# Attention layer of a decoder trunk: order of the indexer's projections and head pairs, place of the top-k selection, engine of the mask and bias sum

## The chip, the cores and the metric

The kernel runs on one core of one Trainium2 chip. The metric is the time of one execution on the device in microseconds (us), as the median of several runs. Five engines run their own instruction streams in order: PE (TensorE, the matmuls, with PEld for its weight loads), DVE (VectorE), ACT (ScalarE), POOL (GpSimd) and SP (SyncE, which here only issues DMAs).

## What is computed

A trunk of two layers over 256 tokens of width 1024, in float32. Each layer has a half-step SwiGLU network, a mixer, and another half-step SwiGLU network, each behind an RMS norm and added to the residual. The mixer of the first layer is a pooling and convolution module, which the change does not touch. The mixer of the second layer is sparse attention:

```
proj = h @ c_w_in                      # q, k, v (16 heads x 64), qi (8 x 64), ki (64), wi (8)
rel   = relu(einsum('thd,sd->ths', qi, ki))
score = einsum('ths,th->ts', rel, wi) * idx_scale, -inf where s > t
sel   = top_k(score, 64)               # 64 of the causal keys for each query
logits = q . k[sel] * attn_scale + rel_bias[t5_bucket(t - sel)], -inf where sel > t
y = softmax(logits) . v[sel] @ c_w_out
```

The kernel computes the logits of all causal keys and adds a mask that removes the keys that are not among the 64 selected.

## The kernel before

All weights are streamed from memory. One float32 weight tile (`raw`) is split into two parts, `hi` (a rounding to the matmul's input type, made by ACT at L158) and `lo` (the rest, `raw - hi`, made by DVE at L182, in one place by POOL). A product is the sum of three matmuls, hi·hi, hi·lo and lo·hi. There are two kinds of weight tile: `gu` (1024 rows of 256 columns, split in two instructions) and `d` (128 rows of 1024 columns, one instruction). `pump(n)` (L170) writes the splits of the next n tiles of the stream into the instruction streams, where a free buffer is at hand; `issue()` then has SP issue the next loads. The author sets the order by hand: what stands earlier in the code stands earlier on each engine, and no scheduler reorders it.

The second layer's mixer, `mixer_c`, runs in this order:

- `wide` (L292) projects the indexer's queries (items 0 and 1, two banks of 128 columns each, `use_qi`) and its keys and weights (item 2, 72 columns, `use_kw`). Its first pass takes the first 128 tokens of all three, its second pass (L312, L315) finishes item 0, 1, 2 in turn. `use_kw` writes `kw` (64 rows of keys, 8 rows of head weights), and POOL issues a DMA that copies the 64 key rows to rows 64 to 127 of another tile, `k2` (L778).
- The loop over eight chunks of V (L823, twelve matmuls each). Behind chunk 0, `index_weights` transposes the head weights (L793). Behind chunks 1 to 4, `index_heads` (L804) computes the scores of two indexer heads, in a block of four small matmuls over 64 rows. Heads with an even number use rows 0 to 63 and `kw`, heads with an odd number rows 64 to 127 and `k2`. The pairs are (0, 2), (4, 1), (6, 3), (5, 7). ACT takes the relu (L807), DVE sums it into `score` (L811, L813).
- Behind chunk 5, `select` (L954) masks the future with POOL (L958) and then runs eight rounds on DVE; each finds and removes the eight largest scores of each query (L968, L969). L972 turns what was removed into the additive `mask`.
- The loop over eight pairs of attention heads, steps s = 0 to 7. Step s projects q and k of pair s (`qk_group`, L268, two groups of 24 matmuls), between them computes the logits of pair s-1 (`logits`, L873, L875), and at its start transposes the probabilities of pair s-2 (L900), at its end multiplies them with V (L912). The bias of a pair is a tile `bm` that `load_bias` loads with two DMAs of POOL's queue (L858); `mask_bias` adds the mask to it with two POOL instructions (L863, L865). DVE adds the biased mask to the logits and takes the row's extreme (L883), ACT takes the exponential (L885), DVE divides by the sum (L889, L891).

Of the kernel before, what the change touches and what calls it, by code (L numbers as in the profile page):

```python
# [11 lines left out]
ALU = mybir.AluOpType  # L12
# [27 lines left out]
def tile_trunk(ctx: ExitStack, tc: tile.TileContext, d: dict, out: bass.AP):  # L40
# [248 lines left out]
            bvs.append(b.rearrange("p (l n) -> p l n", l=2))  # L289
        return bvs  # L290

    def wide(items, finish_b, pumps=True, ahead=2):  # L292

        banks = []
        for n, (w, cols, _) in enumerate(items):
            if n == len(items) - 1:
                finish_b()
            bs = []
            for cs, tag in cols:
                m = cs.stop - cs.start  # L300
                b = bank(tag)
                bv = b[:m].rearrange("p (l n) -> p l n", l=2)
                for c in range(NCH):
                    pe.matmul(bv[:, :, 0:P], w[0][:, c, cs], hT[:, c, 0:2, 0:P],  # L304
                              start=c == 0, stop=False, skip_group_check=True)
                bs.append((bv, cs))
            banks.append(bs)
        pump(ahead)
        for (w, cols, use), bs in zip(items, banks):
            for bv, cs in bs:  # L310
                for c in range(NCH):
                    pe.matmul(bv[:, :, P:2 * P], w[0][:, c, cs], hT[:, c, 0:2, P:2 * P],  # L312
                              start=False, stop=False, skip_group_check=True)
                for c in range(NCH):
                    pe.matmul(bv[:, 0, :], w[1][:, c, cs], hT[:, c, 0, :],  # L315
                              start=False, stop=c == NCH - 1, skip_group_check=True)
            done("gu")
            use([bv for bv, _ in bs])
            if pumps:
                pump(1)  # L320
# [443 lines left out]
    def mixer_c(finish_b, gname):  # L764
# [11 lines left out]
        def use_kw(bvs):  # L776
            wide_sum(bvs[0], 72, kw)
            pool.dma_start(k2[64:128], kw[0:64])  # L778

        two = (slice(0, P), slice(P, 2 * P))  # L780
        wide([(weights("gu"), list(zip(two, ("g0", "g1"))), use_qi(0)),
              (weights("gu"), list(zip(two, ("g2", "g3"))), use_qi(1)),
              (weights("gu"), [(slice(0, 72), "a0")], use_kw)], finish_b)
        g = load_gain(gname)


# [29 lines left out]
        for c in range(NCH):  # L816
# [7 lines left out]
                                  start=c == 0 and n == 0, stop=c == NCH - 1 and n == 2)  # L824
            if c == 0:
                index_weights()
            if 1 <= c <= 4:
                index_heads(((0, 2), (4, 1), (6, 3), (5, 7))[c - 1])
            if c == 5:
                mask = select(score)  # L830
            pump(2)
            done("d")
        v = [[None, None], [None, None]]
        for t in range(2):
            for half in range(2):
# [24 lines left out]

        def mask_bias(j):
            m = biases[j]
            pool.tensor_tensor(m[:, :, 256:384], m[:, :, P:256],  # L863
                               mask[:, None, 256:384].to_broadcast([P, 2, P]), op=ALU.add)
            pool.tensor_tensor(m[:, :, 0:256], m[:, :, 0:256],  # L865
                               mask[:, None, 0:256].to_broadcast([P, 2, 256]), op=ALU.add)

        def logits(j, tags):
            q, k = qk[j, 0], qk[j, 1]
# [46 lines left out]
            dve.tensor_tensor(lo, b[:, 0:256], f32(hi), op=ALU.subtract)  # L916
            kts[j] = (hi, lo)

        load_bias(0)
        for s in range(8):  # L920
            if s >= 2:
                transposes(s - 2, ("a0", "a1"))
            w = weights("gu")
            b = bank(f"g{s % 2}")
            qk_group(s, w, b, 0)
            if s >= 1:
                if s < 8:
                    load_bias(s)
                mask_bias(s - 1)
                logits(s - 1, ("g2", "g3"))  # L930
            pump(1)
            qk_group(s, w, b if s else bank("g2"), 1)
            done("gu")
            if s >= 2:
                values(s - 2, f"b{s % 2}")
# [5 lines left out]
            pump(1)  # L941
            done("d")

        mask_bias(7)
        out_all(0)
        logits(7, ("g2", "g3"))
        out_all(1)
# [215 lines left out]
```

## Time and profile before

| | us |
|---|---|
| median of three runs | 988.77 (988.34 to 989.34) |
| the profiled execution | 987.02 |
| span of the profiled execution, first to last instruction | 985.3 |
| PE busy in the span | 963.4 (98%) |
| DVE, ACT, POOL busy | 658.6, 534.3, 62.3 |

A busy time says how long an engine had an instruction in work. A PE near 98% means that nearly every microsecond of the kernel is a matmul, and that the few idle stretches and slow stretches of PE are what can be read off the trace one by one. The time of other engines counts only where PE waits for them. The timelines give a start and a duration; PE's instructions overlap, so the cost of a block is read from one start to the next start, not from durations.

### The profile page before, as it was taken

To read this page: it belongs to the slowest core of one execution; us is meant where nothing else is said; L and a number is where in the kernel's file an instruction comes from. 1 tells how busy PE (TensorE), PEld (TensorE's weight loads), DVE (VectorE), ACT (ScalarE), POOL (GpSimd) and SP (SyncE) were. 2 spreads that over 40 slices of the span, in tenths; PEclk is the share of its full clock that TensorE was granted. 3 is DMA by queue.
4 is the path that set the end of the run, shared out by engine and by line. 5 is a ranking of instruction groups with operands and counts; after the bars stand their busy time and mean duration, and the time that the engine had idled before them with its cause. 6 is when DMAs were issued, how large, how long until landed. Compare 5 with 4: busy or idle time off the path is not lost.

```text
span 985.3 us, 14682 instructions
## 1 busy us (share of the span) xinstructions
PE 963.4 (98%) x5720; PEld 836.3 (85%) x5720; DVE 658.6 (67%) x1083; ACT 534.3 (54%) x959; POOL 62.3 (6%) x89
## 2 busy tenths in 40 slices
PE   7999999999979999999999999999999999999997
PEld 6888888898869888888988888888899798888885
DVE  6876666678568666666686666667888658666653
ACT  5665555565556645554565555445556556555542
POOL 3000000000000000000000000000435000000000
PEclk9999999999999999999999999999999999999999
DMA  9875555535246757655365555437444527655401
GB/s 335 305 278 186 191 190 188 187 109 181 65 148 230 264 205 244 237 194 190 111 254 192 192 192 193 162 107 279 148 137 151 210 71 253 232 189 191 155 1 43
DMA packets 38021, 182.03 MB, mean 185 GB/s; under 512 B 6416, under 2 KB 6448, under 8 KB 24768
## 3 DMA queue, kind: packets, MB, share of 16 engines
q1 hardware_dynamic: 32400, 169.92, 48.6%
q0 software_dynamic: 5264, 10.92, 3.4%
q8 instruction: 45, 0.74, 0.3%
q10 hardware_dynamic: 288, 0.27, 0.1%
q14 instruction: 24, 0.20, 0.1%
HBM read 179.92 MB, written 4.22 MB: 187 GB/s over the span
## 4 chain that ended last, share of the span: by engine, by line
PE 92%; DVE 4%; ACT 2%; issue 2%; DMA 0%; POOL 0%; SPq 0%; POOLq 0%; DVEq 0%; ACTq 0%
PE g L284 29%; PE g L287 15%; PE a L341 14%; PE b L341 13%; PE g L268 4%; PE g L312 2%; PE g L315 2%; PE g L304 2%; PE a L268 1%; DVE lo L182 1%; PE b L538 1%; PE a L312 1%; PE a L315 1%; PE b L823 1%; DVE keep L969 1%
## 5 line engine op out<-in xcount | busy, mean ns | idle before, releaser
L182 DVE TENSOR_TENSOR lo<-raw,hi 128x1024 fp32r<-128x1024 f32 (+1 forms) x319 | 380.4, 1244 | 57.8 <-ACT hi L158 57.8
L158 ACT CAST hi<-raw 128x1024 fp32r<-128x1024 f32 x320 | 314.7, 1043 | 5.4 <-DMA raw<-in_c_out 2.6
L284 PE MATMUL g<-hT,hi 128*128 128x512 f32 x1248 | 310.7, 391 | 0.8 <-DVE t L327 0.8
L284 PEld LDWEIGHTS g<-hT,hi 128*128 128x128 f32 x1248 | 228.7, 188 | 44.8 <-DVE t L327 1.0
L324 ACT COPY t<-g 128x256 f32<-128x256 f32 x174 | 63.4, 372 | 222.2 <-PE g L287 205.9
L287 PEld LDWEIGHTS g<-hT,lo 128*128 128x128 f32 x1248 | 170.3, 190 | 12.2
L287 PE MATMUL g<-hT,lo 128*128 128x256 f32 x1248 | 174.0, 282 | 0.0
L327 DVE TENSOR_TENSOR t<-g,t 128x256 f32<-128x256 f32 x174 | 71.9, 421 | 137.2 <-ACT t L324 137.0
L341 PE MATMUL a<-hi,kh 128*128 128x512 f32 x208 | 82.7, 398 | 0.0
L341 PE MATMUL b<-hi,kh 128*128 128x512 f32 x208 | 82.6, 397 | 0.0
L341 PE MATMUL a<-lo,kh 128*128 128x512 f32 x208 | 81.9, 394 | 0.0
L341 PE MATMUL b<-hi,kl 128*128 128x512 f32 x208 | 81.5, 392 | 0.0
L341 PE MATMUL b<-lo,kh 128*128 128x512 f32 x208 | 81.5, 392 | 0.0
L341 PE MATMUL a<-hi,kl 128*128 128x512 f32 x208 | 81.0, 389 | 0.0
L392 ACT CAST kh<-t 128x256 fp32r<-128x256 f32 x88 | 35.7, 406 | 57.8 <-DVE t L390 57.8
L393 DVE TENSOR_TENSOR kl<-t,kh 128x256 fp32r<-128x256 f32 x88 | 37.4, 425 | 41.5 <-ACT kh L392 41.5
L388 ACT ACTIVATE t<-t 128x256 f32<-128x256 f32 x88 | 36.9, 420 | 26.1 <-DVE t L327 26.1
L235 POOL TENSOR_TENSOR sm<-sm,mhalf 128x1 f32<-128x1 f32 x11 | 6.1, 554 | 673.2 <-DVE sm L233 673.2
L341 PEld LDWEIGHTS a<-hi,kl 128*128 128x128 f32 x208 | 39.1, 188 | 8.8
L341 PEld LDWEIGHTS b<-hi,kl 128*128 128x128 f32 x208 | 39.3, 189 | 8.3
L341 PEld LDWEIGHTS b<-hi,kh 128*128 128x128 f32 x208 | 39.4, 189 | 8.2
L341 PEld LDWEIGHTS b<-lo,kh 128*128 128x128 f32 x208 | 39.4, 189 | 7.8
(210 smaller groups left out, 949.9 us busy)
## 6 DMA issues: line engine op xcount, KB each, us to landing
raw<-in_gu SPq DMA_DIRECT2D x87, 1024.0 KB, 4.8
raw<-in_dn SPq DMA_DIRECT2D x88, 512.0 KB, 5.3
raw<-in_c_qk SPq DMA_DIRECT2D x8, 1024.0 KB, 4.9
raw<-in_ab_in SPq DMA_DIRECT2D x6, 1024.0 KB, 4.8
raw<-in_ab_out SPq DMA_DIRECT2D x8, 512.0 KB, 5.2
raw<-in_c_v SPq DMA_DIRECT2D x8, 512.0 KB, 4.3
raw<-in_c_out SPq DMA_DIRECT2D x8, 512.0 KB, 4.0
eall<-escr POOLq DMA_DIRECT2D x4, 768.0 KB, 17.3
```

The lines of the kernel that those rows point to most:

```text
L158: act.copy(hi[:, c], raws[k][:, c])
L182: e.tensor_tensor(lo[:, c], raws[k][:, c], f32(hi[:, c]), op=ALU.subtract)
L268: pe.matmul(dst, wt[:, c, cols], hT[:, c, part, :], start=n == 0, stop=n == len(seq) - 1)
L284: pe.matmul(b, hi[:, c, cols], hT[:, c, 0:2, :], start=c == 0, stop=False, skip_group_check=True)
L287: pe.matmul(b[:, 0:256], lo[:, c, cols], hT[:, c, 0, :], start=False, stop=c == NCH - 1, skip_group_check=True)
L312: pe.matmul(bv[:, :, P:2 * P], w[0][:, c, cs], hT[:, c, 0:2, P:2 * P], start=False, stop=False, skip_group_check=True)
L324: act.copy(t[:m], bv[:, 1, :])
L327: dve.tensor_tensor(dst[:m], bv[:, 0, :], t[:m], op=ALU.add)
L341: pe.matmul(acc, kt[a][:, ts], w[b][:, hs], start=start and n == 0, stop=stop and n == 2)
L388: act.activation(s, gv, AF.Silu)
L392: act.copy(hi, m)
L393: dve.tensor_tensor(lo, m, f32(hi), op=ALU.subtract)
```

## The change

Six edits, all in the second layer's mixer and in `wide`:

1. `wide` gets an order for its second pass, here item 2 (keys and head weights), then 0, then 1. The banks are handed out anew: item 2 has `g0`, and the fourth bank of the queries is `a0`. `done` reports a finished weight tile only when all before it are finished.
2. The head pairs are (0, 1), (2, 3), (4, 5), (6, 7), behind chunks 0 to 3.
3. `select` stands behind chunk 3 and behind that chunk's `pump(2)`; a dummy exponential (`preload`) stands ahead of it on ACT.
4. `mask_bias` runs on DVE. It stands one step earlier: the mask of pair 0 ahead of the loop, that of pair s in step s.
5. The biases of pairs 0 and 1 are loaded ahead of the loop, the bias of pair s+1 in step s, behind the logits.
6. Step 0 splits no weight tile, step 1 splits two.

```diff
-    def wide(items, finish_b, pumps=True, ahead=2):
+    def wide(items, finish_b, pumps=True, ahead=2, second=None):
...
-        for (w, cols, use), bs in zip(items, banks):
+        ended = set()
+        for n in second or range(len(items)):
+            (w, cols, use), bs = items[n], banks[n]
...
-            done("gu")
+            before = next(k for k in range(len(items) + 1) if k not in ended)
+            ended.add(n)
+            done("gu", next(k for k in range(len(items) + 1) if k not in ended) - before)
...
-        wide([(weights("gu"), list(zip(two, ("g0", "g1"))), use_qi(0)),
-              (weights("gu"), list(zip(two, ("g2", "g3"))), use_qi(1)),
-              (weights("gu"), [(slice(0, 72), "a0")], use_kw)], finish_b)
+        wide([(weights("gu"), list(zip(two, ("g1", "g2"))), use_qi(0)),
+              (weights("gu"), list(zip(two, ("g3", "a0"))), use_qi(1)),
+              (weights("gu"), [(slice(0, 72), "g0")], use_kw)], finish_b, second=(2, 0, 1))
...
             if c == 0:
                 index_weights()
-            if 1 <= c <= 4:
-                index_heads(((0, 2), (4, 1), (6, 3), (5, 7))[c - 1])
-            if c == 5:
-                mask = select(score)
+            if c < 4:
+                index_heads((2 * c, 2 * c + 1))
             pump(2)
             done("d")
+            if c == 3:
+                preload(AF.Exp)
+                mask = select(score)
...
         def mask_bias(j):
             m = biases[j]
-            pool.tensor_tensor(m[:, :, 256:384], m[:, :, P:256],
-                               mask[:, None, 256:384].to_broadcast([P, 2, P]), op=ALU.add)
-            pool.tensor_tensor(m[:, :, 0:256], m[:, :, 0:256],
-                               mask[:, None, 0:256].to_broadcast([P, 2, 256]), op=ALU.add)
+            dve.tensor_tensor(m[:, :, 256:384], m[:, :, P:256],
+                              mask[:, None, 256:384].to_broadcast([P, 2, P]), op=ALU.add)
+            dve.tensor_tensor(m[:, :, 0:256], m[:, :, 0:256],
+                              mask[:, None, 0:256].to_broadcast([P, 2, 256]), op=ALU.add)
...
-        load_bias(0)
+        for j in range(2):
+            load_bias(j)
+        mask_bias(0)
         for s in range(8):
...
             if s >= 1:
-                if s < 8:
-                    load_bias(s)
-                mask_bias(s - 1)
                 logits(s - 1, ("g2", "g3"))
-            pump(1)
+                if s < 7:
+                    load_bias(s + 1)
+                pump(2 if s == 1 else 1)
+                mask_bias(s)
             qk_group(s, w, b if s else bank("g2"), 1)
...
-        mask_bias(7)
         out_all(0)
```

On PE, the first block of indexer heads. Before, it stands behind chunk 1 of V (`a0` is that chunk's last bank, `b1` the next chunk's first), and both of its heads read `kw`, rows 0 to 63:

```order
L823 MATMUL a0_1231_6594<-hi_1210_6464,hT_90 128x512
L804 MATMUL g1_1243_6643<-kw_6402,t1_1216_6508 128x256
L804 MATMUL g3_1244_6644<-kw_6402,t1_1217_6511 128x256
L804 MATMUL g1_1243_6643<-kw_6402,t1_1216_6508 128x128
L804 MATMUL g3_1244_6644<-kw_6402,t1_1217_6511 128x128
L823 MATMUL b1_1234_6597<-hi_1213_6470,hT_90 128x512
```

Now it stands behind chunk 0, directly behind the transposes of the head weights:

```order
L827 MATMUL a0_1231_6594<-hi_1185_6317,hT_90 128x512
L797 MATMUL g0_1236_6611<-ident_74,kw_6402 128x8 x2
L808 MATMUL g1_1237_6615<-kw_6402,t1_1220_6534 128x256
L808 MATMUL g2_1238_6616<-k2_6403,t1_1220_6534 128x256
L808 MATMUL g1_1237_6615<-kw_6402,t1_1220_6534 128x128
L808 MATMUL g2_1238_6616<-k2_6403,t1_1220_6534 128x128
L827 MATMUL b1_1234_6597<-hi_1210_6464,hT_90 128x512
```

The block moved up by one chunk, and each of its two heads reads its own half of the rows.

On DVE, from the end of the selection (its last round, then the mask) to the first logits (L883, `bm` is the bias), before:

```order
L969 MATCH_REPLACE keep_6778<-sm_6830,keep_6777 128x128
L972 TENSOR_SCALAR keep_6833<-keep_6778 128x384
L182 TENSOR_TENSOR lo_6849<-raw_6725,hi_6847 128x1024
L182 TENSOR_TENSOR lo_6867<-raw_6757,hi_6865 128x1024
L182 TENSOR_TENSOR lo_6911<-raw_6789,hi_6909 128x1024
L883 ISA t_1316_6980,sm_6984<-g_1314_6974,bm_6879 128x128
```

and now:

```order
L975 MATCH_REPLACE keep_6750<-sm_6802,keep_6749 128x128
L978 TENSOR_SCALAR keep_6805<-keep_6750 128x384
L182 TENSOR_TENSOR lo_6833<-raw_6707,hi_6831 128x1024
L182 TENSOR_TENSOR lo_6851<-raw_6739,hi_6849 128x1024
L182 TENSOR_TENSOR lo_6869<-raw_6761,hi_6867 128x1024
L868 TENSOR_TENSOR bm_6881<-bm_6881,keep_6805 128x2x128
L870 TENSOR_TENSOR bm_6881<-bm_6881,keep_6805 128x2x256
L888 ISA t_1314_6976,sm_6980<-g_1312_6970,bm_6881 128x128
```

Three splits stand between mask and logits as before, and the two sums of mask and bias have joined them.

On ACT, from the relu of the last two indexer heads to the first copy of V, before:

```order
L807 ACTIVATE t_1266_6745<-g_1264_6739 128x384
L807 ACTIVATE t_1267_6749<-g_1265_6740 128x384
L158 CAST hi_6753<-raw_6661 128x1024
L158 CAST hi_6785<-raw_6693 128x1024
L158 CAST hi_6847<-raw_6725 128x1024
L158 CAST hi_6865<-raw_6757 128x1024
L837 COPY v_6871<-a_1231_6594 128x512
```

and now:

```order
L811 ACTIVATE t_1263_6727<-g_1261_6721 128x384
L811 ACTIVATE t_1264_6731<-g_1262_6722 128x384
L158 CAST hi_6735<-raw_6544 128x1024
L258 ACT_TABLE_LOAD
L258 ACTIVATE sm_6741<-mhalf 128x1
L158 CAST hi_6757<-raw_6675 128x1024
L158 CAST hi_6831<-raw_6707 128x1024
L158 CAST hi_6849<-raw_6739 128x1024
L158 CAST hi_6867<-raw_6761 128x1024
L842 COPY v_6873<-a_1231_6594 128x512
```

The table load, which stood ahead of the first exponential (L885), is now here, and the copies of V have one more cast ahead of them.

## Rows read from the trace of the kernel before

**Rows 1.** The page: its span, and the chain that ended last by engine.

```profile
span 985.3 us, 14682 instructions
...
PE 92%; DVE 4%; ACT 2%; issue 2%; DMA 0%; POOL 0%; SPq 0%; POOLq 0%; DVEq 0%; ACTq 0%
```

**Rows 2.** Waits of PE: who waited for whom, total us, times, longest us.

```profile
PE a L900 <- DVE t L891: 2.0, 2, 1.1
```

**Rows 3.** PE's timeline, indexer: start us, us, engine, line, operation, tiles, count.

```profile
661.68 1.37 PE L312 MATMUL g<-hT,hi 128*128 128x256 f32 x8
...
669.61 1.10 PE L312 MATMUL a<-hT,hi 128*72 128x256 f32 x8
...
685.75 0.48 PE L804 MATMUL g<-kw,t 64*128 64x256 f32 x1
685.75 0.48 PE L804 MATMUL g<-k,t 64*128 64x256 f32 x1
...
686.60 0.50 PE L823 MATMUL b<-hi,hT 128*128 128x512 f32 x1
...
689.57 1.57 PE L804 MATMUL g<-k,t 64*128 64x256 f32 x8
691.07 0.50 PE L823 MATMUL b<-hi,hT 128*128 128x512 f32 x1
```

**Rows 4.** PE's timeline, the first steps of the attention loop, and a later one.

```profile
708.09 0.70 PE L873 MATMUL g<-t,t 64*128 64x256 f32 x4
...
719.70 0.70 PE L873 MATMUL g<-t,t 64*128 64x256 f32 x4
...
753.25 0.70 PE L873 MATMUL g<-t,t 64*128 64x256 f32 x4
...
757.16 0.87 PE L912 MATMUL b<-t,v 128*64 128x256 f32 x8
757.96 0.88 PE L900 MATMUL a<-ident,t 128*128 128x128 f32 x6
...
761.63 0.70 PE L873 MATMUL g<-t,t 64*128 64x256 f32 x4
```

**Rows 5.** A stretch: length, busy us of five engines, granted clock, DMA share, GB/s.

```profile
715.20:718.70 3.50, 3.50 (x20) 3.50 (x20) 3.17 (x2) 1.09 (x3) 0.95 (x1) 0.56 0.12 46
```

**Rows 6.** DVE's timeline: selection, first logits, and a later pair.

```profile
694.09 0.41 DVE L968 MAX8 sm<-keep 128x8 f32<-128x256 f32 x1
...
705.78 0.36 DVE L972 TENSOR_SCALAR keep<-keep 128x384 f32<-128x384 f32 x1
706.05 5.13 DVE L182 TENSOR_TENSOR lo<-raw,hi 128x1024 fp32r<-128x1024 f32 x3
711.11 0.28 DVE L883 CUSTOM_DVE_ANT_0 t<-g,bm 128x128 f32<-128x128 f32 x1
...
762.70 0.29 DVE L883 CUSTOM_DVE_ANT_0 t<-g,bm 128x128 f32<-128x128 f32 x1 [0.20 <-PE g L875]
...
765.13 0.55 DVE L891 TENSOR_SCALAR t<-t,sm 128x128 f32<-128x128 f32 x2
```

**Rows 7.** DVE's groups from 676 to 694 us: count, busy us, mean ns, idle before.

```profile
L182 DVE TENSOR_TENSOR lo<-raw,hi 128x1024 fp32r<-128x1024 f32 x8 | 9.6, 1230 | 0.0
```

**Rows 8.** POOL: groups from 690 to 775 us, and the copy of the keys.

```profile
L865 POOL TENSOR_TENSOR bm<-bm,keep 128x512 f32<-128x512 f32 x8 | 13.7, 1716 | 0.7
...
L863 POOL TENSOR_TENSOR bm<-bm,keep 128x256 f32<-128x256 f32 x8 | 7.8, 976 | 7.5 <-DVE keep L972 7.4
...
673.02 0.59 POOL L778 DMA_DIRECT2D k<-kw  x1 [14.27 <-DVE kw L327]
```

**Rows 9.** Time to landing: of the bias loads, and of the copied keys.

```profile
DMA to landing us min/median/max: 2.3/2.6/5.0
...
k<-kw POOLq DMA_DIRECT2D x1, 64.0 KB, 5.1
```

**Rows 10.** ACT's timeline, the last cast ahead of the copies of V.

```profile
697.75 1.05 ACT L158 CAST hi<-raw 128x1024 fp32r<-128x1024 f32 x1 [2.57 <-DMA raw<-in_c_out]
```

## The prediction

> **What bounds the kernel now.** I read the page first: the chain that ended last runs over PE for 92% of the span [rows 1], so a change pays only where it takes time from PE, either instructions or waits. The other engines are read only for whether PE waits for them. The list of PE's waits names one in the part that the change touches: L900, the transposes of the first pair's probabilities, waited 2.0 us in two pieces for DVE's division L891 [rows 2]. PE's timeline shows what this wait costs in all. From the logits of pair 0 to those of pair 1, 708.09 to 719.70, PE took 11.61 us; the same stretch of a later step, 753.25 to 761.63, took 8.38, of which the product with V (757.16 to 757.96, 0.80) is not yet there in the early step. So the early step should take 7.58 and takes 4.03 more [rows 4]. The wait itself is 2.0 of that; behind it the granted clock was 0.56 over 3.5 us [rows 5], which is mostly the lower of the two levels, 1.2 instead of 2.4 GHz. The clock fell behind the idle time and rose again under dense matmuls. A waiting time that goes should take its slow stretch along.
>
> What made DVE late is its own queue [rows 6]: the selection runs from 694.09 to the mask at 706.14, then three splits take 5.13 us, and only at 711.11 comes the first L883, though the logits' matmuls began at 708.09. An undisturbed split is 1.23 us [rows 7], three are 3.7; the other 1.4 fell together with POOL's sums of mask and bias [rows 8].
>
> **The indexer's head pairs.** A block whose two heads share the rows took 689.57 to 691.07, 1.50 us; one with heads from both halves took 685.75 to 686.60, 0.85, and the rows show the two halves starting at the same moment [rows 3]. Two of the four blocks, (0, 2) and (5, 7), are of the first kind and become of the second: 2 x 0.65 = **1.3 us less on PE**, which nothing hides. The trace says nothing on a block directly behind the transposes of the head weights; one interruption of the V chunks goes and one change of matmul shape is new, which I take as 0 (from 0.2 lost to 0.2 won).
>
> The Trainium skill, page "TensorEngine Tiling (Array Packing)", section "Theoretical Speedup", gives up to 2x for a contraction of at most 64 rows. By that a block would fall from 1.50 to 0.75 and the sum would be 1.5; the measured block is at 0.85, so the rows' 1.3 stands.
>
> **Keys first.** The first block now needs `kw` and `k2` one chunk earlier, and it needs `k2`, which the old first block did not. The keys' group moves from 669.61 to the place of 661.68, 7.9 us earlier [rows 3]. So the copying DMA goes from 673.02 to about 665.1 [rows 8], and with its 5.1 us to landing [rows 9] the copy is there at 670.2. The blocks' period is 3.82 (685.75 to 689.57); the last block will begin at 685.95 (0.85 for the new first block, 0.65 less for the second), so the first at 685.95 - 3 x 3.82 = 674.5. The cover is 4.3 us: cost nothing. If the landing took 10 us, PE would wait 0.6. The same groups stand in the same passes, so `wide` itself costs what it did; the gain's DMA behind the copy in POOL's queue goes earlier as well.
>
> **The selection.** From the end of the last block to the first maximum it was 691.07 to 694.09, 3.02 us, with relu, sums and one split between; the same instructions stand there now. The last block ends at 685.95 + 0.85 = 686.8, so the selection starts near 689.8 and, 12.05 long [rows 6], gives the mask at 701.9 instead of 706.1. Three undisturbed splits (3.7) bring DVE to 705.6.
>
> **Mask and bias on DVE.** Eight times two sums, 256 and 512 columns, leave POOL (0.98 and 1.72 in the mean [rows 8]) and join DVE. The trace of before has no such sum on DVE. The nearest row is the split: also a float32 difference of two operands in SBUF, 1.23 for 1024 columns [rows 7]; 768 columns are 0.9 at that rate, and with a second start I take 1.1. The ends are 0.9 and POOL's 2.7. With 1.1 DVE is free at 706.7. PE's first logits come at 708.09 - 1.3 = 706.8, and DVE can take them 1.07 later (761.63 to 762.70 [rows 4, 6]), at 707.9, so DVE waits for PE there and not the other way round. From L883 to the end of the last division it is 2.98 (762.70 to 765.13 + 0.55 [rows 6]): 710.8. PE wants the transposes of the first head 3.91 behind the logits (753.25 to 757.96 less 0.80), at 710.7, those of the second 0.3 later, 711.0. It fits with 0.1 to 0.2 to spare; a wait of up to 0.5 here is the likeliest loss. The stall of **4.0 us goes**, and its slow stretch with it.
>
> Behind the sums in DVE's queue wait the next L883, the division and so PE's next transposes. In step 1 three splits and the sums follow the division: 710.8 + 3.7 + 1.1 = 715.6, against logits at 706.8 + 7.58 + 1.07 = 715.4: 0.2 late, where PE leaves 4.71 - 4.05 = 0.66. In a later step the chain from the logits is 4.05 + 2.5 (two splits) + 0.3 (gaps, an estimate from the 0.20 of idle time ahead of L883 in [rows 6]) + 1.1 + 0.4 (the split of the product) = 8.3, against 9.45 (8.38 + 1.07): cost nothing. This cover is gone from 2.2 us for a pair of sums.
>
> **Bias loads, step 0, ACT.** A bias is now loaded a step ahead of its sum, 8.38 us against landings of 2.3 to 5.0 [rows 9]: nothing. What step 0 doesn't split, step 1 does (counted above). On ACT the table load leaves the place ahead of the first exponential, where ACT waited for DVE anyway. New ahead of the copies of V is one more cast, whose tile can only be loaded when POOL has split an earlier one. Before, the last cast there began at 697.75 after 2.57 us of waiting for a load [rows 10]; one more such wait and cast (2.57 + 1.05) puts the copies at 702.4 at worst, which leaves 4.4 us for the copies of V and of q and k until the logits at 706.8. Cost nothing; if it were 3 us later, the logits would be late by about as much.
>
> **The sum.** 1.3 + 4.0 = 5.3, about 5.4 with half of the interruption: the span goes from 985.3 to 979.9. The profiled execution took 987.02, 1.7 over its span and 1.75 under the median; I take the 5.4 off the median: 988.77 - 5.4 = **983.4**.
>
> **Rivals.**
> - *The wait only moves* (0.18). If the first division is late for another reason than the selection (the three splits waiting for casts, the cast for its load, or the sums nearer to 2.7), part of the 4.0 stays. For: 0.2 us of room is little, and three splits still stand between mask and sums. Against: about 4.2 us of lead on DVE. With half of the stall kept 985.4 (0.08), with all of it 988.77 - 1.3 = 987.5 (0.10).
> - *The pairing brings nothing* (0.05): the first block waits for `k2`, or blocks in the new place take 1.5. Then 4.0 alone: 984.8. Against it: the 4.3 us of cover and the two blocks that already run at 0.85.
> - *DVE becomes the bound of the loop* (0.07), the one that ends slower. Place: the sums ahead of each L883. From 2.2 us a pair each step is late by the excess. At POOL's 2.7 it is 0.5 x 7 - 0.66, about 2.8, and the time 986.2. It turns into a loss (over 2 us above before) from about 3.3 a pair; if each of the two took the 1.72 of POOL's longer group, 3.4, it would be 1.2 x 7 - 0.66 = 7.7, with one slow stretch (3.5 x 0.44 = 1.5) 9.2, so 992.6. For: DVE has the longest chain of the loop and POOL's work is put into it. Against: the same kind of operation at 1.23 for 1024 columns, and POOL no longer lengthens DVE's splits.
> - *It doesn't do what it says*: the selection would have to wait for something that the code doesn't show, such as POOL's masking of the future. That is the first rival's case.
>
> **How the numbers follow.** Forecast 983.4 with 0.70, for itself from 982.5 (0.2 more from the interruption, 0.5 scatter of runs) to 984.4. Under 0.2%, 2 us, a measurement of this kernel can't be told from no change. Faster: 0.70 + 0.08 + 0.05 = 0.83. Same: 0.10. Slower: 0.07. The range takes in the half-kept stall (985.4), the missing pairing (984.8) and sums at POOL's price (986.2): 982.3 to 986.2.
>
> **What would show it.** Right: four indexer blocks at 0.85; the mask near 702; no wait of L900 near 711 and no stretch under full clock there; from logits to logits 7.6 in step 1 and 8.4 later; DVE's sums at 0.3 to 0.7 each. Wrong: L883 of pair 0 later than 708.5; a wait of a block for the key copy near 674.5; steps longer than 8.4; or a stall of PE in a place where it had none.

## The result, and the profile after

The changed kernel took 983.61 us in the median of four runs (982.65 to 984.21) against 989.06 for the kernel before on the same chip (988.34 to 989.44). The ratio is 0.995, with a 95% interval from 0.9937 to 0.9963. The forecast was 983.4. So the time was right; the reason was right in part, as the experiments below show.

The profiled execution of the changed kernel took 983.51 us. Its page answers [rows 1] (first fence). PE's list of waits has one in the mixer that was not there before (second fence):

```profile
span 981.7 us, 14669 instructions
...
PE 94%; DVE 2%; ACT 1%; issue 1%; DMA 1%; SPq 0%; POOL 0%; POOLq 0%; DVEq 0%; ACTq 0%
```

```profile
PE b L345 <- DVE kl L921: 0.3, 1, 0.3
```

The wait of [rows 2] is gone. The chain runs over PE for 94% instead of 92%, over DVE for 2% instead of 4%.

PE's timeline (start us, us, engine, line, operation, tiles, count, and in brackets the idle time ahead and who ended it), the lines that answer [rows 3] and [rows 4], and the new wait; L808, L878 and L905 are the former L804, L873 and L900, and L345 is the output product behind the loop of attention pairs:

```profile
676.07 0.48 PE L808 MATMUL g<-kw,t 64*128 64x256 f32 x1
676.08 0.48 PE L808 MATMUL g<-k,t 64*128 64x256 f32 x1
...
676.92 0.50 PE L827 MATMUL b<-hi,hT 128*128 128x512 f32 x1
...
708.12 0.70 PE L878 MATMUL g<-t,t 64*128 64x256 f32 x4
...
711.95 0.82 PE L905 MATMUL a<-ident,t 128*128 128x128 f32 x6
...
715.56 0.70 PE L878 MATMUL g<-t,t 64*128 64x256 f32 x4
...
723.95 0.70 PE L878 MATMUL g<-t,t 64*128 64x256 f32 x4
...
765.43 0.50 PE L345 MATMUL b<-hi,kh 128*128 128x512 f32 x1 [0.26 <-DVE kl L921]
```

The first block of indexer heads takes 0.85 from start to start (676.07 to 676.92), both halves starting together. From the first logits to the second it is 7.44 (before 11.61), then 8.39. The transposes at 711.95 wait for nothing. The granted clock is full where it was 0.56 in [rows 5]; the columns of this row are its stretch, its length, the busy us of PE, PEld, DVE, ACT and POOL, the granted clock, the DMA share and GB/s:

```profile
712.50:721.00 8.50, 8.50 (x74) 7.75 (x73) 7.87 (x20) 6.91 (x17) 1.06 (x2) 1.00 0.61 224
```

DVE's timeline, which answers [rows 6]: the mask (L978), the three splits, the sums of mask and bias (L868, L870), the first logits (L888), and the last pair's sums ahead of a split of a product (L921):

```profile
703.29 0.36 DVE L978 TENSOR_SCALAR keep<-keep 128x384 f32<-128x384 f32 x1
703.57 3.49 DVE L182 TENSOR_TENSOR lo<-raw,hi 128x1024 fp32r<-128x1024 f32 x3
706.97 0.42 DVE L868 TENSOR_TENSOR bm<-bm,keep 128x256 f32<-128x256 f32 x1
707.43 0.69 DVE L870 TENSOR_TENSOR bm<-bm,keep 128x512 f32<-128x512 f32 x1
...
709.08 0.29 DVE L888 CUSTOM_DVE_ANT_0 t<-g,bm 128x128 f32<-128x128 f32 x1 [0.96 <-PE g L880]
...
763.90 0.42 DVE L868 TENSOR_TENSOR bm<-bm,keep 128x256 f32<-128x256 f32 x1
764.35 0.69 DVE L870 TENSOR_TENSOR bm<-bm,keep 128x512 f32<-128x512 f32 x1
764.96 0.42 DVE L921 TENSOR_TENSOR kl<-b,kh 128x256 fp32r<-128x256 f32 x1
```

DVE now stands idle for 0.96 us ahead of the first logits; before, PE waited for DVE. (The first logits of DVE also start 0.96 behind those of PE, 709.08 less 708.12. The two lengths are equal by chance; it is the second that is compared with other runs below.) Its three splits take 3.49 instead of 5.13, and the two sums 1.07 from the first start to the next instruction's.

Two profiled executions can't be compared by their spans alone: the first large product started at 21.05 us in the profile of before and at 22.57 in this one. So I cut the mixer into three stages by the starts of PE's instructions: the V loop (first matmul of V to the first q group), the attention loop (to the first output matmul) and the output stage (to the next network's first matmul). The same kernel run again repeats these lengths to 0.07 us. us:

| kernel | V loop | attention | output | sum | timed: median, ratio to before (95% interval) |
|---|---|---|---|---|---|
| before | 27.89 | 67.61 | 26.69 | 122.19 | 989.06 |
| after | 26.39 | 63.44 | 27.24 | 117.07 | 983.61, 0.995 (0.9937 to 0.9963) |
| again | 26.39 | 63.44 | 27.31 | 117.14 | 984.01, 0.9952 (0.9939 to 0.9966) |
| u_pairs | 27.65 | 63.44 | 27.31 | 118.40 | 983.94, 0.9957 (0.9944 to 0.9971) |
| u_heads | 26.63 | 63.77 | 27.24 | 117.64 | 984.46, 0.9953 (0.9941 to 0.9965) |
| u_sums | 26.39 | 64.27 | 26.69 | 117.35 | 984.59, 0.9955 (0.9938 to 0.9971) |
| u_heads_sums | 26.63 | 65.23 | 26.69 | 118.55 | 984.65, 0.9954 (0.994 to 0.9969) |
| u_step0 | 26.39 | 65.10 | 27.27 | 118.76 | 985.97, 0.997 (0.9957 to 0.9983) |
| b_dve | 27.89 | 64.69 | 26.71 | 119.29 | 985.75, 0.9968 (0.9955 to 0.9981) |
| late3 | 26.39 | 64.97 | 27.28 | 118.64 | 983.46 (one run; before beside it 987.73) |
| late5 | 26.39 | 68.36 | 27.29 | 122.04 | 987.65 (one run; before beside it 987.95) |
| dose2 | 26.39 | 63.49 | 28.19 | 118.07 | 983.79 (one run; before beside it 987.73) |
| dose3 | 26.39 | 66.07 | 31.71 | 124.17 | 989.44 (one run; before beside it 987.73) |
| v2_sum7_late | 26.39 | 63.44 | 26.71 | 116.54 | 982.92, 0.9937 (0.9924 to 0.9949) |

The change is −1.50 in the V loop, −4.17 in the attention loop and +0.55 in the output stage, −5.12 in all, against −5.45 between the medians. Outside of the three stages nothing moved: from the first large product to the first matmul of V it is 650.43 us before and 650.44 after, and from the next network's first matmul to the end of the span 191.6 in both. So the new order in `wide` costs nothing.

### The profile page after: what moved, and what is told of

Read it like the earlier page. It is cut to its first block, busy times and chain, and to the rows that moved or that the text cites. A ratio compares the mean times of both kernels' runs of the same rounds, so it can differ in the third digit from the quotient of the medians.

```text
span 981.7 us, 14669 instructions
## 1 busy us (share of the span) xinstructions
PE 961.3 (98%) x5720; PEld 834.6 (85%) x5720; DVE 653.1 (67%) x1099; ACT 534.2 (54%) x960; POOL 40.7 (4%) x73
## 4 chain that ended last, share of the span: by engine, by line
PE 94%; DVE 2%; ACT 1%; issue 1%; DMA 1%; SPq 0%; POOL 0%; POOLq 0%; DVEq 0%; ACTq 0%
PE g L284 29%; PE g L287 15%; PE a L345 14%; PE b L345 13%; PE g L268 5%; PE g L314 2%; PE g L317 2%; PE g L304 2%; PE a L268 1%; PE b L827 1%; PE a L827 1%; PE b L542 1%; DVE lo L182 1%; PE a L317 1%; PE a L314 1%
## 5 line engine op out<-in xcount | busy, mean ns | idle before, releaser
L182 DVE TENSOR_TENSOR lo<-raw,hi 128x1024 fp32r<-128x1024 f32 (+1 forms) x319 | 371.6, 1217 | 58.5 <-ACT hi L158 58.2
L345 PE MATMUL b<-hi,kh 128*128 128x512 f32 x208 | 82.7, 397 | 0.3 <-DVE kl L921 0.3
L345 PE MATMUL a<-hi,kh 128*128 128x512 f32 x208 | 82.7, 398 | 0.0
L345 PE MATMUL a<-lo,kh 128*128 128x512 f32 x208 | 81.9, 394 | 0.0
L345 PE MATMUL b<-hi,kl 128*128 128x512 f32 x208 | 81.5, 392 | 0.0
L345 PE MATMUL b<-lo,kh 128*128 128x512 f32 x208 | 81.5, 392 | 0.0
L345 PE MATMUL a<-hi,kl 128*128 128x512 f32 x208 | 81.0, 389 | 0.0
L345 PEld LDWEIGHTS b<-hi,kh 128*128 128x128 f32 x208 | 39.4, 189 | 8.8 <-DVE kl L921 0.7
L345 PEld LDWEIGHTS a<-hi,kl 128*128 128x128 f32 x208 | 39.1, 188 | 8.8
L345 PEld LDWEIGHTS b<-hi,kl 128*128 128x128 f32 x208 | 39.3, 189 | 8.3
L345 PEld LDWEIGHTS b<-lo,kh 128*128 128x128 f32 x208 | 39.4, 189 | 7.8
L394 DVE TENSOR_TENSOR t<-t,t 128x256 f32<-128x256 f32 x88 | 37.4, 425 | 11.7 <-ACT t L392 4.2
```

What stands on the lines that cost most here:

```text
L182: e.tensor_tensor(lo[:, c], raws[k][:, c], f32(hi[:, c]), op=ALU.subtract)
L345: pe.matmul(acc, kt[a][:, ts], w[b][:, hs], start=start and n == 0, stop=stop and n == 2)
L394: dve.tensor_tensor(m, s, uv, op=ALU.mult)
```

## The experiments

The medians of most of these kernels lie within one another's intervals; what tells them apart are the stage lengths, which the table gives. All edits are made to the changed kernel, except in b_dve.

**The changed kernel again**, to learn how far a stage repeats.

> The changed kernel once more, as the yardstick for the other kernels on this chip. Theory (two block costs of 0.65 us and one stall of 4.0 us went, one of about 0.5 us is new): 5.3 us under the kernel before, ratio 0.9945; V loop from its first matmul to the first group of q 26.4 us, attention loop 63.4, output stage 27.2. Rival (part of the gain was the start of the profiled execution): the three lengths differ from these by more than 0.2 us.

The stages came out within 0.07 us of the first profile. A difference of 0.2 in a stage can be read; one of 1 us between two medians can't.

**The old head pairs in the new place.**

```diff
-                index_heads((2 * c, 2 * c + 1))
+                index_heads(((0, 2), (4, 1), (6, 3), (5, 7))[c])
```

> The changed kernel with the old head pairs (0,2), (4,1), (6,3), (5,7) in the new places. Theory: two blocks take 1.50 instead of 0.85 us, V loop 26.4 + 1.3 = 27.7; the selection starts 1.0 to 1.3 later, PE's logits as well, so nothing else changes: total 1.3 over the changed kernel. Rival (the pairing also decides whether DVE is in time): 2 us or more over it, with a wait at the first transposes.

PE's timeline shows the first pair as one row of eight matmuls over the same rows, 1.57 long:

```profile
677.40 1.57 PE L808 MATMUL g<-kw,t 64*128 64x256 f32 x8
```

The V loop is 1.26 longer, and the attention loop the same to 0.01. The pairing is worth what [rows 3] gave for it, 2 x 0.65, and nothing else hangs on it. The timed median didn't show it (983.94): runs of this kernel lay between 983.53 and 986.29.

**Head blocks and selection one chunk later.** The lead of the selection, which the prediction took for the reason that the stall ends, is cut.

```diff
-            if c < 4:
-                index_heads((2 * c, 2 * c + 1))
+            if 1 <= c <= 4:
+                index_heads((2 * c - 2, 2 * c - 1))
...
-            if c == 3:
+            if c == 4:
```

> The changed kernel with the four blocks of indexer heads, and the selection behind them, one chunk later (behind chunks 1 to 4, selection behind chunk 4), all else as changed; one of the three splits behind the mask then stands ahead of the selection. Theory (the lead of one chunk is what removes the stall): selection 2.95 later, less one split of 1.15; DVE takes the first logits 0.7 to 1.0 us late, PE waits that long at the first transposes; if the clock falls as before 2 to 2.5 over the changed kernel, if not about 1. Rival (the stall went because POOL no longer sums): within 0.3 of the changed kernel.

The first logits of DVE came 1.50 behind PE's (708.46), 0.54 later than in the changed kernel, where they come 0.96 behind:

```profile
709.96 0.28 DVE L888 CUSTOM_DVE_ANT_0 t<-g,bm 128x128 f32<-128x128 f32 x1
```

```profile
708.46 0.70 PE L878 MATMUL g<-t,t 64*128 64x256 f32 x4
...
712.29 1.14 PE L905 MATMUL a<-ident,t 128*128 128x128 f32 x6
```

The transposes took 1.14 instead of 0.82, and the attention loop grew by 0.33, less than the wait of 0.7 to 1.0 that I expected. The V loop grew by 0.24. The stall didn't come back: most of what DVE lost here was idle time before. The run moves the selection back by one chunk only, with two splits behind the mask instead of three. The old place, behind chunk 5, is in b_dve.

**The sums back on POOL**, in their new place.

```diff
-            dve.tensor_tensor(m[:, :, 256:384], m[:, :, P:256],
+            pool.tensor_tensor(m[:, :, 256:384], m[:, :, P:256],
...
-            dve.tensor_tensor(m[:, :, 0:256], m[:, :, 0:256],
+            pool.tensor_tensor(m[:, :, 0:256], m[:, :, 0:256],
```

> The changed kernel with the sums of mask and bias on POOL again, in their new places. Lengths from the first matmul of V to the next layer's first: 117.1 us changed, 122.2 before. Theory (several edits each make DVE earlier, and any of them is enough): DVE's three splits behind the mask slow to 5 us, but its first logits have 0.96 us to spare and no sum of 1.07 ahead, so the attention loop stays within 0.3 of 63.4; the output stage falls to 26.7, since no sum stands ahead of the split of pair 5; 116.6 to 117.2. Rival (the move off POOL is what removed the stall): attention loop 66 or more.

The attention loop lost 0.83. DVE was in time for the first logits (it still stood idle for 0.52 ahead of them), as expected, but, as I had not expected, its second division fell together with POOL's next sum and took 1.47 (for two instructions), where the first took 0.55. The three views, DVE, POOL and PE:

```profile
710.21 0.55 DVE L896 TENSOR_SCALAR t<-t,sm 128x128 f32<-128x128 f32 x2
...
711.10 1.47 DVE L896 TENSOR_SCALAR t<-t,sm 128x128 f32<-128x128 f32 x2
```

```profile
711.47 0.74 POOL L868 TENSOR_TENSOR bm<-bm,keep 128x256 f32<-128x256 f32 x1
```

```profile
712.36 0.70 PE L905 MATMUL a<-ident,t 128*128 128x128 f32 x3 [0.47 <-DVE t L896]
```

At the same time the output stage won 0.55 back. So the move of the sums is worth 0.28 net in this kernel.

**Both of these together.**

> The changed kernel with two edits undone together: the indexer's blocks and the selection one chunk later, and the sums on POOL. Alone the first cost 0.57 us in the stretch from V to the next layer (117.64 against 117.07), with 0.33 of it in the attention loop. Theory (the two are substitutes, and together they bring the stall back): DVE's two splits slow to 3.5, it is 1 to 1.5 us late at the first logits, the second division collides with POOL's next sum; attention loop 65.5 to 67. Rival (they add up): 63.8 to 64.2.

The loop lost 1.79, more than 0.33 and 0.83 (65.23, a little under the 65.5 to 67 of the theory). Now DVE, in the midst of the first logits, also waits for POOL's sum (first fence), the second division is long again (1.51), and PE's second transposes wait for it:

```profile
709.55 0.42 DVE L888 CUSTOM_DVE_ANT_0 t<-g,bm 128x256 f32<-128x256 f32 x1 [0.87 <-POOL bm L870]
```

```profile
713.04 0.70 PE L905 MATMUL a<-ident,t 128*128 128x128 f32 x3 [1.15 <-DVE t L896]
```

Each of the two edits covers a part of what the other would have left.

**The sums' move alone, in the kernel before.**

```diff
-            pool.tensor_tensor(m[:, :, 256:384], m[:, :, P:256],
+            dve.tensor_tensor(m[:, :, 256:384], m[:, :, P:256],
...
-            pool.tensor_tensor(m[:, :, 0:256], m[:, :, 0:256],
+            dve.tensor_tensor(m[:, :, 0:256], m[:, :, 0:256],
```

> The kernel before with only the sums of mask and bias moved to DVE, in their old places. Theory (POOL's sums lengthened three splits by 1.4 us and a division by 0.95): first logits 0.4 to 0.5 earlier on DVE, still 1.5 late, division undisturbed; the wait falls from 2.0 to 1.2 to 1.4, and if the clock then keeps its level the attention loop goes from 67.6 to 65.0, otherwise to 66.4. Rival (the later place of the selection alone makes the stall): attention loop 67.6.

This is the run that changed my reading. With the old pairs, the late selection and the split in step 0 all in place, the attention loop fell by 2.92 of the 4.17, to 64.69, a little under the 65.0 of the theory. DVE's splits and second division, and PE's transposes, of b_dve:

```profile
707.80 3.49 DVE L182 TENSOR_TENSOR lo<-raw,hi 128x1024 fp32r<-128x1024 f32 x3
...
714.70 0.55 DVE L891 TENSOR_SCALAR t<-t,sm 128x128 f32<-128x128 f32 x2
```

```profile
714.15 0.71 PE L900 MATMUL a<-ident,t 128*128 128x128 f32 x3 [0.32 <-DVE t L891]
715.04 0.70 PE L900 MATMUL a<-ident,t 128*128 128x128 f32 x3 [0.17 <-DVE t L891]
```

and, from the trace of before, what stood there on DVE (besides the 5.13 of [rows 6]), on POOL at that time, and on PE:

```profile
713.53 1.49 DVE L891 TENSOR_SCALAR t<-t,sm 128x128 f32<-128x128 f32 x2
```

```profile
706.22 1.64 POOL L863 TENSOR_TENSOR bm<-bm,keep 128x256 f32<-128x256 f32 x1 [7.44 <-DVE keep L972]
707.95 2.15 POOL L865 TENSOR_TENSOR bm<-bm,keep 128x512 f32<-128x512 f32 x1
...
713.91 0.74 POOL L863 TENSOR_TENSOR bm<-bm,keep 128x256 f32<-128x256 f32 x1
```

```profile
712.99 0.70 PE L900 MATMUL a<-ident,t 128*128 128x128 f32 x3 [0.92 <-DVE t L891]
714.80 0.95 PE L900 MATMUL a<-ident,t 128*128 128x128 f32 x3 [1.11 <-DVE t L891]
```

POOL's sums lay on top of the splits (1.64 more) and on top of the second division (0.94 more). On DVE the same sums cost 1.07, so by this trade DVE is about 0.6 earlier at the first logits (2.41 behind PE's instead of 3.02) and 1.5 at the end of the second division. PE's waits shrank from 0.92 and 1.11 to 0.32 and 0.17, and the granted clock stayed at 1.00 from 711 to 721.5. The Trainium skill, page "SBUF — State Buffer", section "Who interferes with whom", says that a DVE instruction with two inputs in SBUF contends with a GpSimd instruction that reads SBUF. The 5.13 against 3.49 of the splits agrees.

**The split of step 0 back.** 

```diff
-                pump(2 if s == 1 else 1)
+                pump(1)
                 mask_bias(s)
+            else:
+                pump(1)
```

> The changed kernel with one split in step 0 and one in step 1, as before, instead of none and two. Theory (the tile of step 0's split can only be loaded after a split that now stands behind the selection, so its cast and its split are late, and the first logits wait behind them on DVE): DVE takes the first logits 1.5 to 2.5 us late, attention loop 65.5 to 67.5. Rival (it is only one more split of 1.15 against 0.96 to spare): attention loop 63.4 to 63.8.

The loop lost 1.66, the most of any single edit undone, but not on DVE, whose first logits came 0.95 behind PE's (710.99), as in the changed kernel. The theory had DVE late, and its 65.5 to 67.5 lies above the measured 65.10. PE's first logits waited for ACT's copies of q and k (L853):

```profile
710.04 0.70 PE L878 MATMUL g<-t,t 64*128 64x256 f32 x4 [1.59 <-ACT t L853]
```

ACT's timeline shows why:

```profile
702.73 0.39 ACT L853 ACTIVATE t<-g 128x256 f32<-128x256 f32 x1 [0.54 <-PE g L268]
708.66 1.05 ACT L158 CAST hi<-raw 128x1024 fp32r<-128x1024 f32 x1 [5.54 <-DMA raw<-in_c_out]
709.61 0.66 ACT L853 ACTIVATE t<-g 128x256 f32<-128x256 f32 x2
```

The cast of one more tile stands ahead of the copies in ACT's queue and waited 5.54 us for its load, and the copies with it. The edit "no split in the first step" keeps a wait for a transfer out of the way of the first logits. That it frees DVE of 1.2 us isn't what it is worth here.

The load was issued at 705.05, when the first split behind the mask (703.81) was done and its buffer free. In the kernel before, the same cast stood in the same place and waited for nothing, since its tile had been loaded ahead of the mask:

```profile
702.72 1.04 ACT L158 CAST hi<-raw 128x1024 fp32r<-128x1024 f32 x1
```

So the 1.66 is no part of what the change won over the kernel before. With the earlier selection fewer splits stand ahead of it, so the load comes behind the mask; this edit avoids the loss that the other edits would have brought.

**DVE made late by added sums**, once, at the first pair. `mask_again(0)` adds the mask once more to the same bias tile, two instructions of the same shapes, which changes nothing in what is kept.

```diff
         mask_bias(0)
+        for _ in range(5):
+            mask_again(0)
```

late3 has three of them, late5 five. These two, and the two behind them, were run once each.

> The changed kernel with three more pairs of sums on DVE ahead of the loop (the mask is added to the first bias again, which changes nothing in what is kept), 3 x 1.07 us; nothing else is later. DVE has 0.96 to spare there, so it takes the first logits 2.2 us late and PE should wait about 2.1 at the first transposes, in two pieces, as in the kernel before. Theory (a wait of this length takes the clock down behind it): attention loop 63.4 + 2.1 + 1.5 to 2 = 67.0 to 67.6, with a stretch at the lower level behind the wait. Rival (the fall of the clock needs more than this wait): 65.4 to 65.7, clock at its full level.

A repeat right behind another sum costs 0.94, not 1.07. DVE's first logits came 2.72 behind PE's (706.51 to 709.23), 1.76 later than in the changed kernel. PE's loop lost 1.53, but its list of waits holds only 0.78 of that:

```profile
711.11 0.72 PE L912 MATMUL a<-ident,t 128*128 128x128 f32 x3 [0.62 <-DVE t L903]
711.99 0.70 PE L912 MATMUL a<-ident,t 128*128 128x128 f32 x3 [0.16 <-DVE t L903]
```

No slow stretch followed. The wait of 2.1 that I expected did not come about, since the repeats are cheaper than I had put them; whether a longer one brings the slow stretch needed a larger dose.

> The changed kernel with five more pairs of sums on DVE ahead of the loop, 0.94 us each by the run with three (which made DVE 1.65 late and PE wait 0.78, with the clock at its full level). DVE is 3.5 late, PE should wait 2.6 to 2.7 at the first transposes, a little over the 2.0 of the kernel before. Theory (behind a wait of 2 us or more in this place PE runs a stretch at the lower level, which made 2.0 us of the stall of 4.0): attention loop 63.4 + 3.4 + 1.3 to 2 = 68.1 to 68.9. Rival (the fall in the kernel before came with its two separate waits and the matmuls between, or by chance of the moment): 66.7 to 67.0, clock at its full level.

PE's timeline of late5, and the window behind the wait (columns as above):

```profile
713.80 0.72 PE L912 MATMUL a<-ident,t 128*128 128x128 f32 x3 [2.51 <-DVE t L903]
714.67 0.70 PE L912 MATMUL a<-ident,t 128*128 128x128 f32 x3 [0.15 <-DVE t L903]
715.13 3.13 PE L268 MATMUL g<-hT,hi 128*128 128x256 f32 x16
```

```profile
714.50:718.00 3.50, 3.35 (x20) 3.21 (x20) 3.31 (x5) 3.44 (x6) 0.00 (x0) 0.70 0.29 75
```

DVE's lateness alone brought the stall back, with its slow stretch: the 16 matmuls that take 2.16 at full clock took 3.13, and the loop was 4.92 longer than in the changed kernel (68.36, within the 68.1 to 68.9 of the theory), 0.75 longer than before.

**The sums made dearer in every step**: one or two `mask_again(s)` behind each `mask_bias(s)`.

```diff
                 mask_bias(s)
+                for _ in range(2):
+                    mask_again(s)
```

dose2 has one, dose3 two.

> The changed kernel with each pair's sum of mask and bias done twice (the second adds the mask again): 2.1 instead of 1.07 us on DVE for a pair. Theory (DVE bounds the loop only from about 2.2 us a pair, because it stands idle 1.46 ahead of the logits in a later step): the late steps stay at 8.39 from logits to logits; the first two steps lose 0.5 to 0.8 together, the output stage 1.0 (the split of pair 5 waits behind the last sum); attention loop 63.9 to 64.3, output stage 28.3. Rival (DVE already sets the loop): each step longer by 1.07, attention loop 70.

At 2.0 us a pair (1.07 + 0.94) the loop is not touched (63.49). The output stage is: its new wait grew from 0.26 to 1.20, by the 0.94 of the added sum.

```profile
765.27 0.50 PE L345 MATMUL b<-hi,kh 128*128 128x512 f32 x1 [1.20 <-DVE kl L928]
```

> The same with three sums for each pair, 3.2 us on DVE. Theory: now DVE is the bound, 8.39 - 1.46 + 2.13 = 9.06 from logits to logits in the late steps, about 1 lost at the first logits and 1.7 in step 1; attention loop 68.5 to 71, output stage 29.4, slower than the kernel before by some 1 to 3 us. Rival (a chain other than DVE's sets the steps): late steps 8.4 to 8.6.

At 2.94 a pair the late steps took 8.70 instead of 8.39, and the output stage waited 3.30 in one piece:

```profile
741.24 0.70 PE L885 MATMUL g<-t,t 64*128 64x256 f32 x4
...
749.94 0.70 PE L885 MATMUL g<-t,t 64*128 64x256 f32 x4
...
769.94 0.79 PE L345 MATMUL b<-hi,kh 128*128 128x512 f32 x1 [3.30 <-DVE kl L928]
```

The stages sum to 124.17, 1.98 more than before. That is within the 1 to 3 that I expected, but by two misses that cancel: the loop took 66.07 instead of 68.5 to 71, with late steps of 8.70 instead of 9.06, and the output stage 31.71 instead of 29.4, since its wait grew by 3.04 and the granted clock behind it was 0.50 (770.0 to 773.0). The rival in which DVE becomes the bound is real, and it starts at 2.94 − 0.31 = 2.6 us a pair, not at 2.2.

**The last pair's sums later.** In the output stage, four chunks of `out_all(0)` use banks `a` and `b` in turn, and the second bank `b` comes free only when DVE has split the product of pair 5 (L921). That split stands behind the sums of the last pair, which nobody needs yet.

```diff
-                mask_bias(s)
+                if s < 7:
+                    mask_bias(s)
...
+        mask_bias(7)
         out_all(0)
```

> The changed kernel with one line moved: the sum of mask and bias of the last pair stands behind the split of pair 5's product instead of ahead of it. Theory (the output stage of the changed kernel takes 27.24 instead of 26.69 us because bank b1 is freed by a split that waits behind this sum): the wait of 0.26 us goes, output stage 26.7, total 0.5 under the changed kernel. Rival (the output stage waits for the split weights or another bank): the stage stays at 27.2.

On DVE the split of the product now comes first, and PE's bank `b` follows without a wait:

```profile
763.85 0.42 DVE L921 TENSOR_TENSOR kl<-b,kh 128x256 fp32r<-128x256 f32 x1
764.19 0.42 DVE L868 TENSOR_TENSOR bm<-bm,keep 128x256 f32<-128x256 f32 x1
```

```profile
764.73 0.40 PE L345 MATMUL b<-hi,kl 128*128 128x512 f32 x1
764.96 0.39 PE L345 MATMUL b<-hi,kh 128*128 128x512 f32 x1
```

Between these two matmuls lie 0.23 from start to start, where the changed kernel had 0.66 (764.77 to 765.43), and its next one started 0.34 later instead of 0.23: that makes the 0.55, of which the list of waits shows 0.26. The output stage is back at 26.71, and the stages sum to 116.54, the least of all. The median of 982.92 is the lowest as well, though its interval overlaps that of the changed kernel.

## One rule for the first step

The runs give one account of the attention loop's stall. It is read start to start, not from the list of waits: in the changed kernel the transposes start (711.95) before the matmuls ahead of them are modelled to end (710.99 + 1.12), so a listed wait leaves out part of the loss. What PE loses is what DVE's first logits come later than 0.96 behind PE's, plus what the second division takes beyond 0.55, less 0.2 that PE has to spare. Then the clock comes on top, where it fell.

| kernel | first logits of DVE behind PE's | beyond 0.96 | division beyond 0.55 | less 0.2 | loop over 63.44, measured |
|---|---|---|---|---|---|
| u_heads | 1.50 | 0.54 | 0 | 0.34 | 0.33 |
| u_sums | 1.07 | 0.11 | 0.92 | 0.83 | 0.83 |
| u_heads_sums | 1.07, then 0.87 of waiting | 0.98 | 0.96 | 1.74 | 1.79 |
| b_dve | 2.41 | 1.45 | 0 | 1.25 | 1.25 |
| late3 | 2.72 | 1.76 | 0 | 1.56 | 1.53 |
| before | 3.02 | 2.06 | 0.94 | 2.80 | 4.17, clock fell |
| late5 | 4.60 | 3.64 | 0 | 3.44 | 4.92, clock fell |

The 0.2 is the one number that I fitted. In the two rows where the clock fell, 1.4 and 1.5 are left for it. u_step0 is not in the table: its loss came over ACT.

## Why the prediction was right, and where its reason was not

- **Head pairs** (1.3, with up to 0.2 for the interruption): right. The V loop fell by 1.50; u_pairs gives 1.26 for the pairing, u_heads 0.24 for the place of the blocks. All four blocks ran in 0.85 or 0.86. Most of the 0.24 is the interruption of the V chunks that goes, which the prediction took as 0: in PE's timeline of the changed kernel the V matmul ahead of an interruption takes 0.32 to the next start (675.54 to 675.86) and the one behind it 0.34 (676.92 to 677.26), where others take 0.23, so one interruption costs 0.2, the upper end of what the prediction allowed.
- **Keys first** (nothing): right. The copy was issued at 667.06, 9.0 us ahead of the first block, landed 4.0 later, and no block waited.
- **The selection** (4.2 earlier, and so the stall goes): the lead is there. From the start of the V loop to the start of the mask it was 34.30 us before (705.78 less 671.48) and is 30.28 (703.29 less 673.01). The step "so the stall goes" named one cause as the only one. Of the 4.17 that the loop won, the sums' move alone brings 2.92, since it ends the collisions with POOL and with them the fall of the clock; the other edits with the sums still on POOL bring 3.34 (67.61 less 64.27, u_sums). Either ends most of the stall, and neither all of it. In the changed kernel one chunk of the lead is worth 0.33, with the sums on POOL 0.96 (65.23 less 64.27). The lead alone, put into the kernel before, was not run.
- **Sums on DVE** (1.1 a pair): right, 1.07. That POOL lengthened DVE's splits by 1.4 was in the prediction's first part, and its sum counts with undisturbed splits, but it credits the end of the stall to the selection alone, and the second division's 0.94 was not seen: it is why PE's second wait in [rows 2] was the longer one.
- **"Cost nothing"** for these sums failed in one place, by 0.55. I had named what waits behind them in DVE's queue, the logits, the division and the transposes, and even put the split of the product into the chain; but I only asked whether a step of the loop has room for it, not whether the last one does, where PE's next product needs the bank that this split frees. v2_sum7_late shows it by its opposite.
- **Room**: "0.1 to 0.2 to spare" at the first transposes agrees with the 0.2 fitted above. The bound of the loop was put at 2.2 a pair and is 2.6, because DVE's chain in a later step is shorter than it was put: 9.45 − 8.3 = 1.15 of room, where DVE stands idle 1.46 ahead of the logits.
- **Step 0** was counted as a split moved on DVE. What it avoids, 1.66, lies in ACT's queue, where a cast would wait for its load ahead of the copies of q and k. The prediction had looked at such a cast ahead of the copies of V only, and there it was right to count nothing: the copies of V began at 701.38, no later than the 702.4 allowed.
- **Bias loads and table load** (nothing): neither was undone alone. In the kernel before, ACT waited another 1.54 us for DVE behind the table load (708.60 to 709.88), and POOL's first sum waited for the mask, not for a load (7.44, in the fence of b_dve), so neither of the two made the stall.
- **The clock** came back with the wait, as said. The split of the 4.0 into a wait of 2.0 and a slow stretch of 2.0 was off: start to start it is 2.77 and 1.4 (from the first logits to the q group behind the transposes PE took 7.32 against 4.40 in the changed kernel; 0.15 of these 2.92 are transposes that ran slowly). Since both went, the sum didn't notice.

In all 1.50 + 4.17 − 0.55 = 5.12, against the forecast's 5.4. That the time came within 0.2 of the forecast is in part luck: the V loop and the stall each gave 0.1 to 0.2 more than was counted, the output stage took 0.55 that was not counted, and the medians differ by 0.33 more than the stages.

## What to carry to other kernels

When an engine is late, add up all that made it late, and for each long instruction ask what ran beside it; a neighbour's work that slows it can count for more than the order of its queue. An edit that removes a wait may be one of several that each would have done most of it, so undo them one at a time and also try each alone in the old kernel, because the two give different answers. And when work is put into a queue, look for the instruction behind it that frees a buffer, in the last pass of the loop too, where something else begins to want it.

## What the runs showed of the hardware

POOL's sums slow DVE down, and DVE slows POOL's: three splits took 5.13 beside them and 3.49 alone, a pair of divisions 1.47 to 1.51 instead of 0.55, and POOL's own two sums 1.64 and 2.15 beside the splits, where they take 0.74 and 1.41 in most other steps (their means are 0.98 and 1.72 [rows 8]). It isn't always both: in the next step of the kernel before, POOL's longer sum began first (714.74) and kept its 1.41, while DVE's two splits took 3.44 instead of 2.36. On DVE the same two sums take 1.07. I had expected the split to be lengthened, since [rows 6] and [rows 7] showed it, but not that a division of 0.55 grows by 0.9 when a sum of POOL's starts in the midst of it.

PE's granted clock fell for a stretch behind listed waits of 0.92 and 1.11 close together (before, 0.50 from 715.4 to 717.0), of 2.51 (late5, 0.64 from 715.1 to 718.0) and of 3.30 (dose3, 0.50 from 770.0 to 773.0), that is to the lower of its two levels for most or all of these stretches, and it was back at 1.00 after dense matmuls. It stayed at 1.00 behind single waits of 1.15 (u_heads_sums), 1.20 (dose2) and 1.59 (u_step0), and behind 0.62 and 0.16 (late3). Where it fell it added some 1.4 to 1.5 us, so the last part of such a stall is dearer than the first. late5, dose2, dose3 and late3 are one run each, and what decides whether the clock falls was not tested.
